# Down projection: results added from PSUM onto the output tiles, narrow weights two to a buffer, three operand kinds stored whole

## The chip, the cores and the metric

One core of a Trainium2 chip runs the kernel. The metric is the device time of one execution in microseconds. The execution that the profile shows is one of its own, recorded by the hardware profiler.

Engines: PE (TensorE) multiplies, with PEld as its weight load; DVE (VectorE), ACT (ScalarE) and POOL (GpSimd) do elementwise work; SP (SyncE) issues all DMAs here. Each engine works through its instructions in a fixed order.

## The reference

A decoder block on x of 2048 positions by 1024 features, float32: a normalised input goes through a combined projection into gated linear attention and a gated short convolution, whose results are mixed and added to x. Then follows the part that the change concerns:

```
h2 = rmsnorm(x, norm2_g[l])
ffn = (jax.nn.silu(h2 @ w_ffn_gate[l]) * (h2 @ w_ffn_up[l])) @ w_ffn_down[l]
x = x + ffn
...
return rmsnorm(x, norm_f_g)
```

The hidden width D_FF is 2816.

## The kernel before

**Layout.** Features lie on the 128 partitions, positions along the free axis, in four blocks of 512 (PB); a half is two blocks. A large matrix product is made of units. A unit takes a 2 by 2 block of weight tiles and two by two blocks of the right operand (feature halves by position blocks) and computes four result tiles of 128 by 512 with seven products in place of eight, in Winograd's form of Strassen's scheme (PRODUCTS, line 36). Each of the seven pairs one weight combination (A11, S1, S2, A12, S3, S4, A22) with one operand combination (B11, T1, T2, B21, T3, B22, T4).

**Precision.** Every float32 operand is split in two fp32r parts: ACT writes the high part (a copy, line 154), DVE the rest (a subtraction, line 155). One step of a product is three matmuls, high by high, high by low and low by high (lines 399 to 401).

**A unit's weights** (unit_weights, line 376). One DMA loads the four raw quarters into one of two raw buffers. POOL forms S1, S2, S3 and S4 in place and in the single buffer s1 (lines 382, 383, 384, 389). Each of the seven is split into a buffer wq; there are 4 of them, each large enough for a weight of 512 columns by two parts.

**A unit's results** (unit, line 403). The accumulators oa and ob are PSUM banks that several products run on in: oa holds product 0, then adds product 2, then 4, then 6; ob holds product 1 and later adds 5; product 3 has a bank of its own. Between those, results are read out: after products 0, 1 and 2 ACT copies oa, ob, oa to c11, c22, c12 (line 419); products 3, 4 and 5 are followed by a DVE addition onto those (line 423); what oa holds after product 6 is c21, which stays in PSUM. A product that adds on a bank has to wait until the read before it is done. With `into` the copies go straight to given tiles.

**The feed-forward part.** For each half, ffn_up (line 923) runs 11 passes m of two units (gate and up), multiplies the two, and makes the operand kinds for the down projection: B11, B21, B22, in some passes B12, and the differences T1 to T4 on POOL. split_later splits each of them on ACT and DVE, as a background task that takes a step every second product, and stores both parts (512 KB) in DRAM, in s_act.

ffn_down (line 956) goes through the 11 passes in four groups that start at GROUPS = (0, 2, 5, 8): the first holds 2 passes, the others 3. At a group's start the operands of its passes are loaded, seven kinds each, into buffers op (28 of them, seven of which hold y during the down projection); seven loads of the second group are sent ahead (EARLY). Each group then runs four units, one for two output rows d0. Group 0 has weights of 256 columns and writes its results into the tiles y (`into`); groups 1 to 3 have weights of 384 columns, and their results are added onto y after the unit (line 1000): c21 from PSUM by DVE, the others by POOL, except that DVE also takes c12 in the last group of the second half. In groups 1 and 2 the residual x1 is loaded and added on POOL (line 1007). The last group of the first half stores y (finished later); in the second half it takes sums of squares (ACT squares, POOL adds, lines 803 to 809), and its last unit is a function of its own, last_unit, with eight plain products and the final norm.

**Operands stored whole.** For the normalised inputs of the in and up projections the kinds in WHOLE (T3, B22, T4) are already stored as one float32 tile (256 KB) and split after loading, in load_whole (line 568): one ACT and one DVE instruction for each. The other kinds are stored split and loaded by load_pair.

**Order.** The text gives the instructions in program order; a scheduler that plans with a timeline places them in each engine's order, taking earlier ones first among those that it believes ready. issue_after(ins) ties what is traced in its block behind an instruction of the same engine. PE runs unit after unit; raw loads and weight splits run ahead of it as far as buffers allow.

Of the kernel before, what the change touches and what calls it, by code (L numbers as in the profile page):

```python
# [10 lines left out]
F32 = mybir.dt.float32  # L11
# [41 lines left out]
def tile_hymba_block(ctx, tc, x, xt, win, wa, wgu, wout, wffn, wdown, wdown_first, small, out):  # L53
# [48 lines left out]
    def scratch(name, n):  # L102
        return [
            [dram.tile([P, PB], F32, name=f"{name}{b}_{i}") for i in range(n)] for b in range(NB)
        ]

    s_kq, s_d, s_v, s_g = scratch("sk", 4), scratch("sd", 2), scratch("sv", 4), scratch("sg", 4)
    s_x1 = scratch("sx", KD)
# [4 lines left out]
            {  # L113
                n: dram.tile([P, 2, PB], F32, name=f"sa{half}_{m}_{n}")
                for n in ("B11", "B12", "B21", "B22", "T1", "T2", "T3", "T4")
# [5 lines left out]
    s_h2 = {n: [dram.tile([P, PB], F32, name=f"sf{n}_{k}") for k in range(4)] for n in LATER}  # L121

    def made_ahead(name, n):
        return dram.tile([P, PB] if n in WHOLE else [P, 2, PB], F32, name=name)

# [222 lines left out]
    def plain_unit(src, ops):  # L348
# [12 lines left out]
        return us  # L361

    def weight_quarter(src):
        n = src.shape[-1]
        h = wqp.tile([P, 2, PB], F32R, name="wq", tag="wq")[:, :, 0:n]
        split(src, h[:, 0, :], h[:, 1, :])
        return h
# [7 lines left out]

    def unit_weights(src):
        raw = raw_weights(src)
        n = src.shape[-1]
        a11, a12, a22, a21 = [raw[:, i, :] for i in range(4)]
        s1 = rawp.tile([P, PB], F32, name="s1", tag="s1", bufs=1)[:, 0:n]  # L380
        w = {"A11": weight_quarter(a11)}
        pool.tensor_tensor(s1, a21, a22, ALU.add)  # L382
        pool.tensor_tensor(a21, a11, a21, ALU.subtract)  # L383
        pool.tensor_tensor(a11, s1, a11, ALU.subtract)  # L384
        w["S1"] = weight_quarter(s1)
        w["S2"] = weight_quarter(a11)
        w["A12"] = weight_quarter(a12)
        w["S3"] = weight_quarter(a21)
        pool.tensor_tensor(a12, a12, a11, ALU.subtract)  # L389
        w["S4"] = weight_quarter(a12)  # L390
        w["A22"] = weight_quarter(a22)
        return w

# [8 lines left out]

    def unit(src, ops, into=None):


        w = unit_weights(src)

        def mul(i, o=None):
# [6 lines left out]
            return o  # L415

        def copied(name, o, at):
            t = tt(name) if into is None else into[at]
            act.activation(t[:], o[:], AF.Copy)  # L419
            return t  # L420

        def plus(t, o):
            dve.tensor_tensor(t[:], o[:], t[:], ALU.add)  # L423
            return t
# [13 lines left out]
        mul(6, oa)  # L438
        if into is not None:
            copied("c21", oa, (1, 0))  # L440
# [499 lines left out]
    def split_later(dst, values):  # L940

        for n, y in values:
            store_split(dst[n], y)
            yield

# [5 lines left out]
    def act_op(half, m, n):  # L951
        o = opp.tile([P, 2, PB], F32R, name="op", tag="op")
        load(o[:].bitcast(F32), s_act[half][m][n][:])
        return o

    def ffn_down(half):
# [6 lines left out]
        for u, m0 in enumerate(GROUPS):  # L963
            ms = range(m0, m0 + (3 if u else 2))
            last = m0 == LAST_GROUP
            if last:
                drain_background()
            ops = {n: [group_op(m, n) for m in ms] for _, n in PRODUCTS}
            if last and half:
# [4 lines left out]
            for d0 in range(0, KD, 2):  # L974
# [19 lines left out]
                if last and half and d0 == KD - 2:  # L994
                    last_unit(src, ops, [act_op(half, m, "B12") for m in ms], y, ssq)
                    break
                for r, j, c, p in unit(src, ops):
                    yy = y[d0 + r, j]
                    eng = dve if p or last and half and r != j else pool
                    eng.tensor_tensor(yy, c[:], yy, ALU.add)  # L1000
                    if last and half:
                        sum_squares(ssq[j], yy, j not in begun)
                        begun.add(j)
                    elif last:
                        store(s_x1[2 * half + j][d0 + r][:], yy)
# [216 lines left out]
```

## Time and profile before

| | us |
|---|---|
| median of 3 runs | 2104.45 |
| lowest, highest | 2103.83, 2107.36 |
| the profiled execution, its own time | 2106.52 |
| its span, first to last instruction | 2104.4 |
| busy: PE, PEld, DVE, ACT, POOL | 2036.8, 1656.3, 1415.8, 998.6, 973.1 |

In the span, the up projection of the first half runs from about 745 to 1180 us and its down projection to about 1400; the second half's up projection follows to about 1835 and its down projection to the end. DMA queues moved 456 MB, all issued by SP.

How to read the lines of the profile: a group or timeline row names the line of the kernel, the engine, the operation, and output<-inputs by tile name (numbers of buffers left out), with partitions by elements, and xN for N instructions. Behind a bar or in brackets stands idle time of the engine just before the instructions, and what ended it: [5.83 <-POOL s L382] is 5.83 us of waiting that ended when POOL's instruction of line 382 on tile s did. Lines 154 and 155 are the helper that splits, so the tile name tells what is split: wq a weight, op an operand, so a result to be stored. In the rows by stage, (xN) is the number of instructions, and the last three numbers are PE's granted clock as a share of full speed, the busy share of the DMA engines and GB/s.

### The profile page before, as it was taken

The page shows a single profiled execution, that of the slowest core. Times are in us where ns is not written, and L with a number is a line of the kernel's source. Part 1 is how long each engine was busy: PE and PEld are TensorE (multiplying, and loading weights), DVE is VectorE, ACT ScalarE, POOL GpSimd, SP SyncE. Part 2 cuts the span into 40 slices and gives each one's busy share as a digit, 9 for nine tenths or more (in the row PEclk, how much of TensorE's full clock was granted, in tenths as well). Part 3 has the DMA queues.
Part 4 walks back from the last instruction along what each step waited for, and adds up shares of the span by engine and source line. Part 5 has one row for each costly group of instructions (what it writes and reads, how often), then busy time and mean ns, then how long its engine had stood idle before and what let it go on. Part 6 is the DMA issues. An engine that isn't in the chain of part 4 may idle for free.

```text
span 2104.4 us, 27023 instructions
## 1 busy us (share of the span) xinstructions
PE 2036.8 (97%) x9193; PEld 1656.3 (79%) x9193; DVE 1415.8 (67%) x2018; ACT 998.6 (47%) x1982; POOL 973.1 (46%) x704
## 2 busy tenths in 40 slices
PE   6999999999999999999999999999999999999996
PEld 4768888877888878788888878787888878877775
DVE  7669786549743786787786665557766677575554
ACT  6555455656542355445444443334544544443343
POOL 3436222222102564464464448865545544437773
PEclk9999999999999999999999999999999999999998
DMA  7349385425686862655545687695554544687672
GB/s 279 127 169 315 130 339 160 147 80 175 201 282 242 316 245 106 232 193 212 212 166 191 260 327 269 235 338 225 188 199 169 200 173 169 221 341 261 240 277 98
DMA packets 189241, 458.14 MB, mean 218 GB/s; under 512 B 19824, under 2 KB 65072, under 8 KB 179504
## 3 DMA queue, kind: packets, MB, share of 16 engines
q1 hardware_dynamic: 189104, 456.43, 60.1%
q8 instruction: 72, 1.18, 0.2%
q14 instruction: 65, 0.53, 0.1%
HBM read 294.34 MB, written 162.00 MB: 217 GB/s over the span
## 4 chain that ended last, share of the span: by engine, by line
PE 72%; DVE 7%; DMA 6%; issue 3%; ACT 2%; POOL 2%; SPq 1%; DVEq 0%; ACTq 0%; POOLq 0%
PE mm L399 20%; PE mm L401 20%; PE mm L400 20%; PE mm L827 3%; PE mm L828 2%; PE mm L830 2%; DVE wq L155 2%; DVE so L155 1%; DMA raw<-in_wdown_dram 1%; DMA op<-sa_T 1%; DMA x<-sx 1%; POOL y L1000 1%; ACT wq L154 1%; DMA sa_T<-so 1%; PE o_ps L751 1%
## 5 line engine op out<-in xcount | busy, mean ns | idle before, releaser
L399 PE MATMUL mm<-op,wq 128*128 128x512 f32 x2499 | 980.7, 394 | 20.1 <-ACT wq L154 8.4
L400 PE MATMUL mm<-op,wq 128*128 128x512 f32 x2499 | 975.8, 391 | 0.7 <-DVE op L155 0.7
L401 PE MATMUL mm<-op,wq 128*128 128x512 f32 x2499 | 965.5, 392 | 10.7 <-DVE wq L155 10.0
L155 DVE TENSOR_TENSOR wq<-raw,wq 128x512 fp32r<-128x512 f32 (+2 forms) x626 | 526.5, 848 | 335.8 <-ACT wq L154 333.4
L154 ACT ACTIVATE wq<-raw 128x512 fp32r<-128x512 f32 (+2 forms) x626 | 363.3, 587 | 551.5 <-PE mm L401 389.8
L399 PEld LDWEIGHTS mm<-op,wq 128*128 128x128 f32 x2499 | 470.8, 188 | 133.9 <-ACT wq L154 14.4
L401 PEld LDWEIGHTS mm<-op,wq 128*128 128x128 f32 x2499 | 470.5, 188 | 119.4 <-DVE wq L155 20.8
L400 PEld LDWEIGHTS mm<-op,wq 128*128 128x128 f32 x2499 | 470.9, 188 | 97.5 <-DVE op L155 1.3
L384 POOL TENSOR_TENSOR raw<-s,raw 128x512 f32<-128x512 f32 (+2 forms) x97 | 127.8, 1318 | 419.2 <-DVE wq L155 398.9
L423 DVE TENSOR_TENSOR c<-mm,c 128x512 f32<-128x512 f32 x267 | 183.0, 685 | 93.2 <-PE mm L401 91.1
L382 POOL TENSOR_TENSOR s<-raw 128x512 f32<-128x512 f32 (+2 forms) x97 | 129.1, 1331 | 212.0 <-DMA raw<-in_wffn_dram 88.0
L389 POOL TENSOR_TENSOR raw<-raw 128x512 f32<-128x512 f32 (+2 forms) x97 | 124.7, 1286 | 126.5 <-DVE wq L155 119.2
L419 ACT ACTIVATE c<-mm 128x512 f32<-128x512 f32 x267 | 154.7, 585 | 36.0 <-PE mm L401 34.5
L809 POOL TENSOR_TENSOR ssx<-ssx,q 128x512 f32<-128x512 f32 x52 | 76.2, 1477 | 154.4 <-ACT q L808 154.3
L383 POOL TENSOR_TENSOR raw<-raw 128x512 f32<-128x512 f32 (+2 forms) x97 | 136.7, 1409 | 4.1
L1000 POOL TENSOR_TENSOR y<-c,y 128x512 f32<-128x512 f32 x66 | 98.9, 1501 | 58.2 <-DVE c L423 56.3
L155 DVE TENSOR_TENSOR so<-t,so 128x512 fp32r<-128x512 f32 x96 | 93.2, 976 | 24.3 <-ACT so L154 24.2
L154 ACT ACTIVATE wq<-s 128x512 fp32r<-128x512 f32 (+2 forms) x97 | 56.8, 585 | 97.4 <-PE mm L401 85.0
L827 PE MATMUL mm<-op,wq 128*128 128x512 f32 x256 | 100.9, 395 | 0.0
L828 PE MATMUL mm<-op,wq 128*128 128x512 f32 x256 | 99.7, 389 | 0.0
L155 DVE TENSOR_TENSOR wq<-s,wq 128x512 fp32r<-128x512 f32 (+2 forms) x97 | 79.9, 823 | 15.1 <-ACT wq L154 14.5
L830 PE MATMUL mm<-op,wq 128*128 128x512 f32 x256 | 79.8, 390 | 0.0
(185 smaller groups left out, 1871.8 us busy)
## 6 DMA issues: line engine op xcount, KB each, us to landing
raw<-in_wffn_dram SPq DMA_DIRECT2D x44, 1024.0 KB, 6.4
sa_T<-so SPq DMA_DIRECT2D x88, 512.0 KB, 5.9
op<-sa_T SPq DMA_DIRECT2D x88, 512.0 KB, 9.5
sa_B<-so SPq DMA_DIRECT2D x69, 512.0 KB, 3.4
op<-sa_B SPq DMA_DIRECT2D x69, 512.0 KB, 9.2
raw<-in_win_dram SPq DMA_DIRECT2D x23, 1024.0 KB, 5.4
raw<-in_wdown_dram SPq DMA_DIRECT2D x24, 768.0 KB, 6.1
sx<-y SPq DMA_DIRECT2D x48, 256.0 KB, 3.1
```

What stands on the lines that cost most here:

```text
L154: last_hi[:] = [act.activation(hi, src, AF.Copy)]
L155: return dve.tensor_tensor(lo, src, hi.bitcast(F32), ALU.subtract)
L382: pool.tensor_tensor(s1, a21, a22, ALU.add)
L383: pool.tensor_tensor(a21, a11, a21, ALU.subtract)
L384: pool.tensor_tensor(a11, s1, a11, ALU.subtract)
L399: pe.matmul(o[:], wh, xh, start=first and k == 0, stop=False, skip_group_check=True)
L400: pe.matmul(o[:], wh, xl, start=False, stop=False, skip_group_check=True)
L401: return pe.matmul(o[:], wl, xh, start=False, stop=k == n - 1, skip_group_check=True)
L419: act.activation(t[:], o[:], AF.Copy)
L423: dve.tensor_tensor(t[:], o[:], t[:], ALU.add)
L827: pe.matmul(o[e, j][:], wh, m[:, 0, :], start=k == 0, stop=False)
L828: pe.matmul(o[e, j][:], wh, m[:, 1, :], start=False, stop=False)
```

## The change

Three parts, and what goes with them:

- In groups 1 to 3 of the down projection unit gets `onto`: DVE adds each of the seven readings of PSUM straight onto the y tile. The copies into c and the later additions on POOL are gone from these groups. The squares, stores and residual additions that follow are the same.
- A weight of 256 columns takes half of a buffer wq, and the next one the other half. A half that is left at the end of a unit isn't used.
- T3, B22 and T4 of the down projection's operands are stored whole in DRAM and loaded by load_whole, which splits them. split_later stores these three first, straight from where they were computed, then splits and stores the others one step at a time. Two functions move up in the text for that.
- In groups 1 to 3 the raw weights of the first unit are loaded ahead of the group's operands, whose loads are tied behind it.

```diff
@@ -104,6 +104,9 @@
             [dram.tile([P, PB], F32, name=f"{name}{b}_{i}") for i in range(n)] for b in range(NB)
         ]
 
+    def made_ahead(name, n):
+        return dram.tile([P, PB] if n in WHOLE else [P, 2, PB], F32, name=name)
+
     s_kq, s_d, s_v, s_g = scratch("sk", 4), scratch("sd", 2), scratch("sv", 4), scratch("sg", 4)
     s_x1 = scratch("sx", KD)
     s_mix = [[dram.tile([P, 2, PB], F32, name=f"sm{b}_{k}") for k in range(4)] for b in range(NB)]
@@ -111,7 +114,7 @@
     s_act = [
         [
             {
-                n: dram.tile([P, 2, PB], F32, name=f"sa{half}_{m}_{n}")
+                n: made_ahead(f"sa{half}_{m}_{n}", n)
                 for n in ("B11", "B12", "B21", "B22", "T1", "T2", "T3", "T4")
             }
             for m in range(NF // 2)
...
@@ -360,9 +360,18 @@
                 us.append((r, j, settled(o, True), False))
         return us
 
+    halves = []
+
     def weight_quarter(src):
+
         n = src.shape[-1]
-        h = wqp.tile([P, 2, PB], F32R, name="wq", tag="wq")[:, :, 0:n]
+        if halves:
+            h = halves.pop()
+        else:
+            h = wqp.tile([P, 2, PB], F32R, name="wq", tag="wq")
+            if n == PB // 2:
+                halves.append(h[:, :, n:])
+            h = h[:, :, 0:n]
         split(src, h[:, 0, :], h[:, 1, :])
         return h
 
@@ -373,8 +382,8 @@
         raw_loads.append(load(raw, src))
         return raw
 
-    def unit_weights(src):
-        raw = raw_weights(src)
+    def unit_weights(src, raw=None):
+        raw = raw_weights(src) if raw is None else raw
         n = src.shape[-1]
         a11, a12, a22, a21 = [raw[:, i, :] for i in range(4)]
         s1 = rawp.tile([P, PB], F32, name="s1", tag="s1", bufs=1)[:, 0:n]
@@ -389,6 +398,7 @@
         pool.tensor_tensor(a12, a12, a11, ALU.subtract)
         w["S4"] = weight_quarter(a12)
         w["A22"] = weight_quarter(a22)
+        halves.clear()
         return w
 
     def product_step(o, w, op, k, first):
@@ -400,10 +410,11 @@
         pe.matmul(o[:], wh, xl, start=False, stop=False, skip_group_check=True)
         return pe.matmul(o[:], wl, xh, start=False, stop=k == n - 1, skip_group_check=True)
 
-    def unit(src, ops, into=None):
-
-
-        w = unit_weights(src)
+    def unit(src, ops, into=None, onto=None, raw=None):
+
+
+
+        w = unit_weights(src, raw)
 
         def mul(i, o=None):
             first = o is None
@@ -414,13 +425,15 @@
             tick()
             return o
 
+        def plus(t, o):
+            dve.tensor_tensor(t[:], o[:], t[:], ALU.add)
+            return t
+
         def copied(name, o, at):
+            if onto is not None:
+                return plus(onto[at], o)
             t = tt(name) if into is None else into[at]
             act.activation(t[:], o[:], AF.Copy)
-            return t
-
-        def plus(t, o):
-            dve.tensor_tensor(t[:], o[:], t[:], ALU.add)
             return t
 
 
@@ -436,7 +449,7 @@
         mul(5, ob)
         plus(c12, ob)
         mul(6, oa)
-        if into is not None:
+        if into is not None or onto is not None:
             copied("c21", oa, (1, 0))
         return [(0, 0, c11, False), (1, 1, c22, False), (0, 1, c12, False), (1, 0, oa, True)]
 
@@ -940,8 +953,12 @@
     def split_later(dst, values):
 
         for n, y in values:
-            store_split(dst[n], y)
-            yield
+            if n in WHOLE:
+                store(dst[n][:], y[:])
+        for n, y in values:
+            if n not in WHOLE:
+                store_split(dst[n], y)
+                yield
 
     def store_split(dst, y):
         o = bx[1].tile([P, 2, PB], F32R, name="so", tag="so")
@@ -949,9 +966,7 @@
         store(dst[:], o[:].bitcast(F32))
 
     def act_op(half, m, n):
-        o = opp.tile([P, 2, PB], F32R, name="op", tag="op")
-        load(o[:].bitcast(F32), s_act[half][m][n][:])
-        return o
+        return (load_whole if n in WHOLE else load_pair)(s_act[half][m][n])
 
     def ffn_down(half):
 
@@ -965,7 +980,13 @@
             last = m0 == LAST_GROUP
             if last:
                 drain_background()
-            ops = {n: [group_op(m, n) for m in ms] for _, n in PRODUCTS}
+            raw = None
+            if u:
+                raw = raw_weights(wdown[4 * u - 4])
+                with tc.issue_after(raw_loads[-1].ins):
+                    ops = {n: [group_op(m, n) for m in ms] for _, n in PRODUCTS}
+            else:
+                ops = {n: [group_op(m, n) for m in ms] for _, n in PRODUCTS}
             if last and half:
                 begun = set()
                 ssq = [
@@ -994,10 +1015,10 @@
                 if last and half and d0 == KD - 2:
                     last_unit(src, ops, [act_op(half, m, "B12") for m in ms], y, ssq)
                     break
-                for r, j, c, p in unit(src, ops):
-                    yy = y[d0 + r, j]
-                    eng = dve if p or last and half and r != j else pool
-                    eng.tensor_tensor(yy, c[:], yy, ALU.add)
+                onto = {(r, j): y[d0 + r, j] for r in range(2) for j in range(2)}
+                unit(src, ops, onto=onto, raw=None if d0 else raw)
+                for r, j in ((0, 0), (1, 1), (0, 1), (1, 0)):
+                    yy = onto[r, j]
                     if last and half:
                         sum_squares(ssq[j], yy, j not in begun)
                         begun.add(j)
```

2 lines of the change are left out of this document (removed).

## The prediction

> **What bounds the kernel now.** I read the page's first lines, then PE's busy time by stage, then the timelines of the few stretches where PE is not full.
>
> ```profile
> span 2104.4 us, 27023 instructions
> PE 2036.8 (97%) x9193; PEld 1656.3 (79%) x9193; DVE 1415.8 (67%) x2018; ACT 998.6 (47%) x1982; POOL 973.1 (46%) x704
> ```
>
> PE is busy for 97% of the span, and the change leaves every matmul in place. What can be won is the rest, 2104.4 - 2036.8 = 67.6 us, and only the part of it that lies where the change works. The stages (columns: stretch, its length, busy time and instructions of PE, PEld, DVE, ACT, POOL, then the granted clock, the DMA share, GB/s):
>
> ```profile
> 745.00:1180.00 435.00, 428.27 (x1869) 350.99 (x1869) 330.65 (x384) 215.45 (x373) 231.75 (x155) 1.00 0.52 188
> 1240.00:1390.00 150.00, 148.99 (x653) 121.51 (x652) 80.58 (x114) 54.61 (x109) 109.93 (x86) 1.00 0.75 287
> 1600.00:1700.00 100.00, 100.00 (x443) 82.79 (x442) 65.94 (x78) 46.87 (x83) 55.23 (x38) 1.00 0.49 173
> ```
>
> The third row is the yardstick: 443 matmuls in 100.00 us without a gap, 0.2257 us each. In any stretch, length minus matmuls times 0.2257 is PE time lost, including the slow restart after a gap. Groups 1 to 3 of the first half's down projection (second row) lose 1.0 us of idle time in 150: there is little to win there. The losses that the change can reach are these:
>
> ```profile
> 835.00:855.00 20.00, 17.13 (x67) 13.36 (x66) 20.00 (x27) 12.37 (x22) 10.89 (x7) 0.91 0.59 213
> 1225.00:1235.00 10.00, 7.69 (x31) 5.35 (x30) 5.72 (x10) 4.27 (x11) 4.63 (x6) 1.00 0.48 192
> 1870.00:1880.00 10.00, 7.69 (x31) 5.36 (x30) 6.58 (x11) 4.99 (x12) 4.91 (x6) 1.00 0.47 189
> 1920.00:1930.00 10.00, 8.25 (x36) 6.39 (x35) 4.72 (x6) 2.57 (x6) 9.92 (x9) 1.00 0.37 129
> 1960.00:1970.00 10.00, 8.26 (x27) 5.86 (x26) 2.08 (x4) 1.80 (x4) 5.67 (x5) 0.83 1.02 407
> 2030.00:2040.00 10.00, 7.41 (x33) 5.68 (x32) 5.35 (x10) 5.69 (x11) 5.82 (x5) 1.00 0.38 154
> ```
>
> By the yardstick: 835 to 855 loses 20 - 67 x 0.2257 = 4.9 us (DVE is busy for all of it); the end of group 0 loses 3.0 us in each half (1225, 1870); the second half's later groups lose 1.9, 3.9 and 2.6 us. That is 19.3 us in all.
>
> **The change part by part.**
>
> Narrow weights, two to a buffer. Group 0 of the down projection has weights 256 wide and products of 6 matmuls, 1.35 us. With 4 buffers a weight can be split once the product four before it has ended: it has three products, 4.1 us, of lead. In pairs, the seven weights of a unit fill four buffers, so the next unit's first pair is free after product 1 of this one and leads by five products, 6.8 us. The raw weight buffer is also released earlier, by about those three products. What PE waits for there:
>
> ```profile
> 1226.62 0.50 PE L399 MATMUL mm<-op,wq 128*128 128x512 f32 x1 [0.78 <-DVE y L423]
> 1229.80 0.50 PE L399 MATMUL mm<-op,wq 128*128 128x512 f32 x1 [1.51 <-ACT wq L154]
> ```
>
> Two thirds of the idle time is a weight that came late, which more lead answers; the other third is an eviction into y, which it does not. Of 3.0 us per half I take 2.0: **-4.0 us** for both (bounds: 0, if the raw load is what is late, and -6.0).
>
> Additions off POOL. The groups that change:
>
> ```profile
> L1000 POOL TENSOR_TENSOR y<-c,y 128x512 f32<-128x512 f32 x66 | 98.9, 1501 | 58.2 <-DVE c L423 56.3 <-DMA x<-sx 1.8
> L423 DVE TENSOR_TENSOR c<-mm,c 128x512 f32<-128x512 f32 x267 | 183.0, 685 | 93.2 <-PE mm L401 91.1 <-ACT c L419 0.7
> L419 ACT ACTIVATE c<-mm 128x512 f32<-128x512 f32 x267 | 154.7, 585 | 36.0 <-PE mm L401 34.5
> ```
>
> There are 12 units less the last one of group 3 in the second half: 23. Each drops three ACT evictions (1.8 us) and its additions from c (three, 4.5 us of POOL; in the last group of the second half one of them is DVE's), and gains up to three DVE evictions from PSUM (2.1 us). POOL and ACT do not bound, so the busy time itself is worth nothing; what counts is who queued behind it:
>
> ```profile
> 1917.79 1.54 POOL L1000 TENSOR_TENSOR y<-c,y 128x512 f32<-128x512 f32 x1 [1.80 <-DMA x<-sx]
> 1919.30 2.53 POOL L1007 TENSOR_TENSOR y<-x,y 128x512 f32<-128x512 f32 x2
> 1924.40 0.53 ACT L154 ACTIVATE wq<-s 128x384 fp32r<-128x384 f32 x1 [5.83 <-POOL s L382]
> 1964.86 0.52 ACT L154 ACTIVATE wq<-raw 128x384 fp32r<-128x384 f32 x1 [2.97 <-DMA raw<-in_wdown_dram]
> 2031.67 0.63 ACT L805 ACTIVATE ssx<-y 128x512 f32<-128x512 f32 x1 [2.17 <-POOL y L1000]
> ```
>
> At 1920 the weight sum s stands on POOL behind the additions. Two L1000 additions leave that chain (about 3 us), the residual additions L1007 and their loads stay; of 1.9 us I take 1.5. At 1960 the wait is a raw load landing while the DMA engines are full; fewer bytes per operand help it a little: 1.0 of 3.9. At 2030 a square on ACT waits for the POOL addition, and weight splits and evictions stand behind it on ACT; after the change y comes straight from DVE and no eviction is on ACT: 2.0 of 2.6. With 0.5 of the first half's 1.0 us the term is **-5.0 us** (bounds 0 and 1.9 + 3.9 + 2.6 + 1.0 = -9.4).
>
> Evictions onto y by DVE. Two more matmul groups per unit now wait for a DVE read of their bank: product 2 for that of product 0, product 4 for that of product 2. The slack is one product, 9 x 0.2257 = 2.03 us, against 0.685 us and whatever stands before it on DVE (lo parts of weights and operands, which wait for ACT). PE's own waits give the price:
>
> ```profile
> PE mm L399 <- ACT c L419: 7.0, 6, 2.6
> PE mm L399 <- DVE c L423: 2.5, 2, 1.9
> PE mm L399 <- DVE y L423: 1.6, 2, 0.8
> ```
>
> One in three L423 instructions holds a bank back, 89 gates for 2.5 us, 0.028 us each; on y in group 0 it is 8 gates for 1.6 us, 0.2 each; on ACT 178 gates for 7.0 us, 0.039 each. The 46 moved gates therefore cost between 46 x (0 - 0.039) = -1.8 and 46 x 0.2 = 9.2 us. DVE's load after the change is nearest to that of the up projection (330.65 of 435 us, 76%): 80.58 us in 150, plus some 30 evictions at 0.685 and 18 operand splits at 0.84, is 116, or 78%. So I take the c row: **+1.3 us**.
>
> Three kinds stored whole. In the up projection 66 splits go (ACT and DVE each), their stores and later loads halve to 256 KB, and 66 splits come back behind the loads at the start of the down groups: nine at each of six starts, six at each of two. Rows:
>
> ```profile
> L155 DVE TENSOR_TENSOR so<-t,so 128x512 fp32r<-128x512 f32 x96 | 93.2, 976 | 24.3 <-ACT so L154 24.2
> L155 DVE TENSOR_TENSOR op<-op 128x512 fp32r<-128x512 f32 x24 | 19.6, 842 | 0.0
> L154 ACT ACTIVATE op<-op 128x512 fp32r<-128x512 f32 x24 | 14.2, 622 | 1.2 <-DMA op<-shT 1.2
> op<-sa_T SPq DMA_DIRECT2D x88, 512.0 KB, 9.5
> ```
>
> Up: per pass of two units DVE loses 3 x 0.976 = 2.9 us, which is worth something only where DVE is full: of the 4.9 us at 835 I take 2.0, and 1.0 for the small gaps later: **-3.0 us** (bounds 0 and -6.0). The whole stores wait on SP for POOL's differences with later loads behind them; raw loads run about a unit ahead of their use, so I cost that at nothing, and if that lead is gone it is one late raw load as at 1960, 3.9 us.
>
> Down: the trace of before has two starts with twelve whole operands each. Out of the first I quote the stretch, out of the second the stretch and PE's waits in it:
>
> ```profile
> 265.00:305.00 40.00, 40.00 (x198) 32.20 (x197) 30.83 (x51) 23.59 (x55) 8.70 (x7) 1.00 1.02 394
> 1435.00:1455.00 20.00, 17.61 (x76) 13.86 (x76) 17.49 (x24) 13.42 (x25) 7.46 (x6) 1.00 0.47 179
> PE mm L399 <- ACT c L419: 1.7, 1, 1.7
> PE mm L400 <- DVE op L155: 0.7, 1, 0.7
> PE mm L399 <- ACT op L154: 0.3, 1, 0.3
> ```
>
> The first cost PE nothing, the second 1.0 us on the operands and 2.7 with the eviction that was late behind them. For twelve operands then 0 to 2.7 us; scaled to nine or six, 66/12 = 5.5 such starts: 0 to 14.8 us. DVE, at 54% in these groups before, has spare time that the second start (87%) had not, so I go to between the two plain prices, 0.58 per twelve: **+3.2 us**.
>
> Raw weights ahead of operands. At the second start of a group in the first half:
>
> ```profile
> 1288.10 0.33 SPq L146 DMA_DIRECT2D raw<-in_wdown_dram  x1
> 1291.05 0.32 SPq L146 DMA_DIRECT2D op<-sa_B  x1
> ```
>
> The raw load already goes first, since its buffer comes free earlier than the operands' buffers. The 21 operand loads that are now tied behind it lose nothing: 0.
>
> Sum: -4.0 - 5.0 + 1.3 - 3.0 + 3.2 = **-7.5 us**. Against the profiled span that is 2096.9; the run that was profiled took about 2 us more than its span and lies within the 2103.83 to 2107.36 of the three runs, so I subtract from the median, 2104.45: **2097.0 us**.
>
> A rule that bears on the splits: the Trainium skill, "SBUF — State Buffer", section "Who interferes with whom", says that a DVE instruction with two inputs in SBUF and a GpSimd instruction that reads SBUF exclude each other for a whole instruction. Both the removed additions and the new operand splits are of that kind, an eviction from PSUM is not. By it a split that meets one POOL instruction would cost up to its own time and 1.5 us more, nine of them about 14 us more per start, and the sum would come out slower. The measured 842 ns mean speaks for few such meetings.
>
> **The rivals.**
>
> Slower: ACT and DVE blocked at the head of their queues by a late operand. The operand's hi split stands in ACT's order behind its load, with the weights of the coming products and, on DVE, the evictions behind it; before, only PE waited for these loads, and no PE wait on them shows. For it: loads take 9.5 us in the median, DMA is full at the starts, the 1435 start lost 2.7 us. Against it: ACT waited 1.2 us in all for 24 such loads. At 2.7 us for each of eight starts: -12.0 + 1.3 + 21.6 = +10.9, or 2115 us. It decides once a start loses more than (12.0 - 1.3)/8 = 1.3 us.
>
> No change: the losses in the down groups only move to the next late thing, the raw load at 1960 or the residual loads at 1920. Then the first two terms fall away: -3.0 + 1.3 + 3.2 = +1.5, or 2106 us. For it: two of the five down losses end in a DMA. Against it: the 2030 loss does not.
>
> Larger gain: every bound of the gains, no price at the starts: -6.0 - 9.4 - 6.0 + 1.3 = -20.1, or 2084 us. For it speaks the first start (265), against it that DVE gets busier.
>
> **How the numbers follow.** Forecast 0.46, slower 0.29, no change 0.15, larger gain 0.10. A run can tell about 0.2%, 4.2 us, from no change. Faster holds the larger gain and nearly all of the forecast: 0.55; within: the rest and the no-change case, 0.16; slower 0.29. The forecast's own range, with its gains or its prices at half their way to the bounds, is 2089 to 2105. The range over the cases runs from 2086, which leaves out part of the larger gain, to 2115, the price of the slower case.
>
> **What would show it.** Right: no idle time before wq at the end of group 0 in either half; no L1000-like additions on POOL and ACT's squares no longer waiting for POOL near 2030; DVE near 78% in the down groups and PE waits on its evictions under 2 us in all; op splits (66 more) with little waiting for DMA. Wrong: ACT idle until an op load at the group starts, with PE waits on wq behind it; PE waits for DVE evictions of half a microsecond and more in many units; a DVE mean for op splits well over 1 us.

## The result, and the profile after

The changed kernel takes 2089.69 us in the median of 4 runs (2087.49 to 2091.39) against 2105.9 us (2103.83 to 2109.0) for the kernel before on the same chip: a ratio of 0.9915 with a 95% interval of 0.9898 to 0.9932. By the ratio that is 17.9 us less, between 14.3 and 21.5; the two medians lie 16.2 us apart. The forecast had 7.5 us: the sign is right, the time is within the range (2086 to 2115), the gain was set at less than half.

The page's first lines after:

```profile
span 2085.4 us, 26960 instructions
PE 2029.7 (97%) x9193; PEld 1656.5 (79%) x9193; DVE 1429.7 (69%) x2084; ACT 965.5 (46%) x1913; POOL 881.3 (42%) x638
```

The two spans differ by 19.0 us. Of that, 11.9 us are idle time of PE (67.6 to 55.7 us). The other 7.1 us are busy time, though the matmuls are the same: some ran slower. Up to 2.9 us of it is the clock, which was granted at half for six stretches, 34.7 us in all, before and for five, 28.9 us, after.

To see where, I ordered PE's matmuls by their start in the timeline of each profile and compared the start of the n-th; in the feed-forward part all kernels here run the same matmuls in the same order, but for two to four neighbouring pairs in the second up projection. The stages below are bounded by such numbers, which run 11 ahead of a matmul's place among the 9193 of the trace. First seven stretches of before (columns as in the prediction; in order, to within a few matmuls: 3800 to 4400, 5480 to 5600, 5600 to 6200, 8200 to 8400, 8520 to 8560, 8680 to 8720, 8900 to 9040), then the same matmuls after:

```profile
829.99:973.48 143.49, 138.92 (x602) 113.44 (x601) 110.19 (x134) 73.70 (x127) 73.42 (x49) 0.99 0.60 214
1220.24:1250.74 30.50, 28.19 (x121) 22.16 (x120) 18.04 (x31) 14.61 (x34) 9.55 (x11) 1.00 0.71 266
1250.74:1389.30 138.56, 137.55 (x601) 112.06 (x600) 73.92 (x103) 48.93 (x98) 105.34 (x82) 1.00 0.73 280
1846.95:1896.72 49.77, 47.29 (x201) 36.88 (x200) 35.46 (x57) 25.13 (x56) 19.35 (x20) 1.00 0.86 337
1924.30:1935.72 11.42, 9.67 (x41) 7.12 (x40) 5.84 (x9) 4.91 (x10) 8.47 (x9) 1.00 0.07 23
1963.31:1976.19 12.88, 11.26 (x41) 8.56 (x40) 4.35 (x6) 3.32 (x7) 8.19 (x7) 0.87 0.91 364
2017.37:2052.33 34.96, 32.37 (x141) 26.04 (x140) 18.03 (x25) 18.34 (x35) 22.54 (x19) 1.00 0.61 239
```
```profile
832.76:973.22 140.46, 137.30 (x602) 112.31 (x600) 99.54 (x123) 66.84 (x115) 72.28 (x50) 1.00 0.54 192
1218.88:1246.09 27.21, 27.21 (x121) 22.53 (x120) 16.55 (x30) 12.78 (x29) 8.74 (x11) 1.00 0.65 243
1246.09:1384.26 138.17, 137.58 (x601) 112.05 (x600) 106.23 (x161) 49.85 (x96) 70.44 (x55) 1.00 0.64 233
1842.06:1888.28 46.22, 45.63 (x202) 37.47 (x201) 35.93 (x58) 23.37 (x53) 20.34 (x20) 1.00 0.80 297
1915.47:1924.54 9.07, 9.07 (x41) 7.51 (x40) 4.68 (x10) 2.13 (x5) 3.86 (x3) 1.00 0.19 59
1951.95:1962.22 10.27, 9.87 (x42) 7.20 (x40) 10.27 (x11) 6.00 (x12) 6.76 (x5) 1.00 0.45 172
2003.19:2035.59 32.40, 32.37 (x142) 26.05 (x140) 27.36 (x40) 21.84 (x41) 18.00 (x15) 1.00 0.44 161
```

The end of group 0 (second row), the stretch that was at 1920 (fifth) and the one at 2030 (last) now run practically without a gap. In the third row DVE is busy for 106.23 of 138.17 us, 77%, and PE still idles for only 0.6 us.

PE's waits for the high part of a weight in the whole profile before (one row); three rows of PE's waits in the whole profile after; and its only wait after around the end of the first half's group 0 (1190 to 1250 us):

```profile
PE mm L399 <- ACT wq L154: 8.4, 7, 1.7
```
```profile
PE mm L409 <- ACT c L436: 3.6, 4, 1.7
PE mm L409 <- DVE y L429: 1.5, 4, 0.6
PE mm L409 <- ACT wq L154: 1.5, 2, 1.2
```
```profile
PE mm L409 <- DVE y L429: 0.6, 1, 0.6
```

Waits of a product's first matmul for the high part of a weight fell from 8.4 to 1.5 us, for ACT's copies from 7.0 to 3.6. The new evictions onto y hold PE for 1.5 us in all. The groups that carry the change:

```profile
L429 DVE TENSOR_TENSOR y<-mm,y 128x512 f32<-128x512 f32 x185 | 126.9, 687 | 83.7 <-PE mm L411 83.3
L1028 POOL TENSOR_TENSOR y<-x,y 128x512 f32<-128x512 f32 x32 | 53.1, 1658 | 46.3 <-DVE y L429 37.4 <-DVE op L155 4.5 <-DMA x<-sx 4.3
L155 DVE TENSOR_TENSOR op<-op 128x512 fp32r<-128x512 f32 x90 | 74.1, 850 | 3.3 <-ACT op L154 3.2
L154 ACT ACTIVATE op<-op 128x512 fp32r<-128x512 f32 x90 | 52.5, 621 | 7.3 <-DMA op<-sa_T 3.9 <-DMA op<-shT 1.4 <-DMA op<-sa_B 1.3
op<-sa_T SPq DMA_DIRECT2D x44, 512.0 KB, 7.1
```

DVE reads PSUM onto y 185 times in place of 47 (24 in group 0 and 23 in line 1000), the 66 POOL additions from c are gone, and there are 66 more op splits, at 0.85 us on DVE; before all 90 op splits together ACT waited 7.3 us, mostly for their loads. The loads of split operands land in 7.1 us, down from 9.5.

### The profile page after: what moved, and what is told of

Read it like the earlier page. It is cut to its first block, busy times and chain, and to the rows that moved or that the text cites. A ratio compares the mean times of both kernels' runs of the same rounds, so it can differ in the third digit from the quotient of the medians.

```text
span 2085.4 us, 26960 instructions
## 1 busy us (share of the span) xinstructions
PE 2029.7 (97%) x9193; PEld 1656.5 (79%) x9193; DVE 1429.7 (69%) x2084; ACT 965.5 (46%) x1913; POOL 881.3 (42%) x638
## 4 chain that ended last, share of the span: by engine, by line
PE 80%; DVE 6%; DMA 3%; ACT 2%; issue 1%; POOL 1%; SPq 0%; DVEq 0%; ACTq 0%; POOLq 0%
PE mm L409 24%; PE mm L411 24%; PE mm L410 24%; PE mm L840 1%; PE mm L841 1%; PE mm L843 1%; DVE op L155 1%; DVE wq L155 1%; DVE h L536 1%; DMA op<-shT 1%; PE o_ps L764 1%; PE o_ps L766 1%; DMA ee<-sd 0%; DMA sm<-hi 0%; DVE y L429 0%
## 5 line engine op out<-in xcount | busy, mean ns | idle before, releaser
L155 DVE TENSOR_TENSOR wq<-raw,wq 128x512 fp32r<-128x512 f32 (+2 forms) x626 | 508.7, 818 | 281.0 <-ACT wq L154 278.5
L429 DVE TENSOR_TENSOR c<-mm,c 128x512 f32<-128x512 f32 x198 | 135.8, 686 | 76.9 <-PE mm L411 75.0
L429 DVE TENSOR_TENSOR y<-mm,y 128x512 f32<-128x512 f32 x185 | 126.9, 687 | 83.7 <-PE mm L411 83.3
L436 ACT ACTIVATE c<-mm 128x512 f32<-128x512 f32 x198 | 115.4, 586 | 16.1 <-PE mm L411 14.4
L155 DVE TENSOR_TENSOR wq<-s,wq 128x512 fp32r<-128x512 f32 (+2 forms) x97 | 84.9, 875 | 2.9 <-ACT wq L154 2.1
L155 DVE TENSOR_TENSOR op<-op 128x512 fp32r<-128x512 f32 x90 | 74.1, 850 | 3.3 <-ACT op L154 3.2
```

Source lines behind the costliest of these rows:

```text
L155: return dve.tensor_tensor(lo, src, hi.bitcast(F32), ALU.subtract)
```

## The experiments

Each table entry is the length of a stage in one profile minus its length in the kernel before (first column, us), worked out from the matmul starts as above. "control" is the kernel before profiled again: it shows by how much two profiles of one kernel differ, 1.0 us at most in the up projections and 0.4 us in the down projections. Stages up to matmul 6480 belong to the first half of the positions (the end of its last group and the load of the second half's operands lie in 6200 to 6480), the later ones to the second half. A star marks a stage in which that kernel ran one stretch at half clock, explained below the table.

```
matmuls     what             before  | control  after | pairs   onto    whole  | whole+onto no_whole no_pairs
3800-5200   up projection     326.2* |   1.0    -4.4  |  -0.1*   0.0    -4.4   |   -4.4       0.7*    -3.7*
5200-5600   group 0            94.6  |   0.1    -3.0  |  -2.2    0.1     1.5   |    0.9      -2.2      0.9
5600-6200   groups 1 to 3     138.6  |   0.0    -0.4  |   1.0   -1.4     3.5   |    0.0      -1.9     -0.5
6200-6480   end, next half     67.3  |  -0.4     1.3  |  -0.4   -0.7     2.7*  |    0.1      -0.7      0.3
6480-8200   up projection     390.6  |  -0.2    -1.4  |   0.9*   1.4    -1.4   |   -1.1       1.0*    -0.7
8200-8400   group 0            49.8  |   0.0    -3.5  |  -2.7    1.6*    0.4   |    1.0      -2.2      0.4
8400-8680   group 1, 2         66.6  |   0.0    -3.1  |  -0.8   -3.1    -1.0   |   -2.6      -2.0     -2.0
8680-8720   (was 1963)         12.9* |   0.0*   -2.4  |  -2.5   -3.1    -1.8   |   -2.5      -3.1     -2.5
8720-8900   group 2, 3         41.2  |   0.0     0.0  |  -0.1   -0.4     0.6   |    0.1      -0.4      0.1
8900-9040   group 3            35.0  |   0.0    -2.6  |   1.6*  -3.0     0.5   |   -2.6      -3.0     -2.6
3800-9040                    1222.6  |   0.7   -19.5  |  -5.2   -8.6     0.6   |  -11.1     -13.8    -10.2
measured ratio                       |         0.9915 | 0.9974 0.9965  0.9997  |  0.9955     0.9932   0.9944
```

Ratios are to the kernel before on the same chip, whose median was 2105.9 to 2109.4 us; all intervals are within 0.0017 of the ratio on either side.

**Stretches at half clock.** Now and then the granted clock fell to a half for 3.41 us, which costs 1.7 us where PE is busy. In the stages of the table there are 17 such stretches in the sixteen profiles, and each follows right on 3.41 us in which PE was idle for 1.5 to 2.6 us. The first two rows are of before, the loss at 1963 (PE busy for 1.68 of 3.40 us, clock 1.00) and what follows it (clock 0.50); the third is of before after its gap of 2.6 us near 2039, the fourth of copies_dve, a kernel described below, after its gap at the same place, 2.7 us. At full clock 16 matmuls fall into such a row, at half 8 or 10:

```profile
1962.90:1966.30 3.40, 1.68 (x6) 0.79 (x6) 1.51 (x2) 0.52 (x1) 1.48 (x2) 1.00 1.02 408
1966.30:1969.70 3.40, 3.40 (x8) 2.75 (x9) 0.00 (x0) 0.00 (x0) 3.03 (x3) 0.50 1.03 404
2041.40:2044.80 3.40, 3.40 (x16) 2.81 (x16) 0.90 (x1) 2.58 (x5) 2.66 (x3) 1.00 0.36 144
2038.90:2042.30 3.40, 3.40 (x10) 2.65 (x9) 1.10 (x3) 0.89 (x2) 1.95 (x2) 0.51 0.47 186
```

So a gap of one size can cost 1.7 us more or not, and a stage that differs by about that much may differ in the clock alone. The changed kernel has no such stretch in these stages, the kernel before has two: 3.4 of the 19.5 us are the clock, 1.7 of them the loss at 1963 and 1.7 in the first up projection. Control has none in that projection and is no shorter there, so the second 1.7 us can't be booked as a lasting gain.

**One part alone: only_pairs, only_onto, only_whole.** Each is the kernel before with the lines of one part of the diff: `halves` in weight_quarter and unit_weights; `onto` in unit and ffn_down; made_ahead for s_act, split_later and act_op. The core of each:

```diff
+            if n == PB // 2:
+                halves.append(h[:, :, n:])
...
+            if onto is not None:
+                return plus(onto[at], o)
...
+        return (load_whole if n in WHOLE else load_pair)(s_act[half][m][n])
```

> The kernel before with only the pairing of narrow weights. Theory (the forecast's step, with the size that the trace after shows): the end of group 0 loses about 3 us less in each half, nothing changes elsewhere: -6 us, ratio near 0.997. Rival: at the end of group 0 the gain comes from fewer split instructions and bytes (operands stored whole), so pairing alone gives within 1 us of before.

> The kernel before with only the additions from PSUM onto y by DVE. Theory: the second half's groups 1 to 3 lose 8 to 10 us less (the stretches that began at 1920, 1960 and 2030 in the kernel before), group 0 and the up projection stay: -9 us. Rival: the stretch at 1960 belongs to the operand loads and stays, and evictions that wait on DVE take some back: -4 us.

> The kernel before with only the three kinds stored whole (no raw load moved). Theory: the up projection of the first half gains 4 us and the group starts cost 0 to 3 us: -4 to -1 us. Rival 1: the group starts gain too, since 22% fewer bytes stand before the raw loads: -8 us. Rival 2 (the forecast's slower case): ACT and DVE are held at the group starts: +3 us or more.

Pairing: 0.9974 (0.9964 to 0.9984), and the two group 0 stages lose 4.9 us as the theory said. Additions from PSUM: 0.9965 (0.9952 to 0.9978), 7.4 us; the stages that were named are 9.6 us shorter, and the second half's group 0, with a stretch at half clock, is 1.6 us longer. Storing whole: 0.9997 (0.9987 to 1.0007), and the table shows why it is nothing: the first up projection gains 4.4 us, as expected, and the first half's down projection gives 1.5, 3.5 and 2.7 us back, 7.6 in all, 1.7 of it half clock; the second half's stages gain 2.7 in all.

The three parts together would give 0.9974 x 0.9965 x 0.9997 = 0.9936, 13.5 us; the change gives 0.9915. With these intervals the ratios alone hardly tell the two apart, but the table does: in the first half's groups 0 to 3 (5200 to 6200), where control agrees to 0.1 us and nothing ran at half clock, the parts alone add up to +2.4 us and the change gives -3.4. They are not independent.

One thing fits no theory: only_pairs, which touches neither POOL nor the loads of groups 1 to 3, is 2.5 us shorter at 1963 (1.7 of it the half clock that is not there) and, between matmuls 8520 and 8560, the stretch at 1920, 1.5 us shorter too. only_whole, which leaves the additions on POOL, is even 2.4 us shorter between 8520 and 8560, all that was lost there. POOL's timeline in that stretch, first the weight sum in the kernel before (three of the four instructions ahead of it are in the prediction), then only_pairs:

```profile
1923.36 1.01 POOL L382 TENSOR_TENSOR s<-raw 128x384 f32<-128x384 f32 x1
```
```profile
1914.62 1.30 POOL L1009 TENSOR_TENSOR y<-c,y 128x512 f32<-128x512 f32 x1
1917.02 1.54 POOL L1016 TENSOR_TENSOR y<-x,y 128x512 f32<-128x512 f32 x1 [1.09 <-DVE y L1009]
1918.52 1.28 POOL L1009 TENSOR_TENSOR y<-c,y 128x512 f32<-128x512 f32 x1
1919.78 1.32 POOL L390 TENSOR_TENSOR s<-raw 128x384 f32<-128x384 f32 x1
```

The same work stands in another order, with matmul 8520 at nearly the same time (1924.2 and 1924.3): the sum s starts at 1919.78, behind two additions in a row, not at 1923.36 behind four. The order that the scheduler made shifted with the earlier stage.

**The kernel before once more: control.** No edit.

> The kernel before, unchanged, for a second profile of it. If the losses of the second half's groups 1 and 2 (the stretches at 1920 and 1960) belong to the kernel, they are there again, 2 and 3.5 us. If they belong to that one execution, they are not, and what the change gained there was never the additions' doing.

2110.15 us in its one execution, and the two stretches are there again to within 0.1 us, the half clock at 1963 too. So they belong to the kernel before and not to one execution of it. At 1920 the order of instructions, which different edits move, is shown above; at 1963 what every edit takes away is first of all the half clock.

**Which queue matters: adds_dve and copies_dve.**

```diff
adds_dve:
-                    eng = dve if p or last and half and r != j else pool
+                    eng = dve
copies_dve (units of groups 1 to 3 only):
-            act.activation(t[:], o[:], AF.Copy)
+            dve.tensor_copy(t[:], o[:])
```

> The kernel before with the additions of line 1000 all on DVE, still from c, and the ACT copies kept. If what helps is that POOL no longer stands before the weight sums and the squares, this gives most of the gain of adding from PSUM, -6 us or more, although DVE does 66 more instructions of two SBUF inputs. If the ACT copies and the longer way over c matter, it gives 0 to -2 us, or a loss by DVE's load.

> The kernel before, with the copies to c in groups 1 to 3 of the down projection made by DVE in place of ACT; the additions stay on POOL. If the loss near 2030 comes from evictions that stand on ACT behind the squares (and weight splits), it goes here, 2.5 us between matmuls 8900 and 9040. If it comes from the squares' wait for POOL's additions, it stays. In all -5 to 0 us.

adds_dve: 0.9988 (0.9977 to 0.9998), between the two expectations; it gains 1.9 and 2.3 us at the two stretches above but only 0.5 in group 3. copies_dve: 0.9995 (0.9983 to 1.0007), and group 3 is 1.8 us longer, not 2.5 shorter; 1.7 of that is half clock, so the loss itself simply stays. PE's waits near there, first of adds_dve (2018 to 2059 us), then of copies_dve (2015 to 2057 us):

```profile
PE mm L399 <- ACT c L419: 3.3, 2, 2.2
```
```profile
PE mm L399 <- DVE c L420: 3.0, 2, 2.7
```

The wait for the copy follows the copy to whichever engine makes it. The timeline shows why. In the kernel before, out of the rows of DVE, ACT and PE:

```profile
2035.53 0.63 ACT L808 ACTIVATE q<-y 128x512 f32<-128x512 f32 x1 [1.78 <-DVE y L1000]
2037.37 0.57 DVE L155 TENSOR_TENSOR wq<-raw,wq 128x384 fp32r<-128x384 f32 x1 [1.87 <-ACT wq L154]
2037.86 0.68 DVE L1000 TENSOR_TENSOR y<-mm,y 128x512 f32<-128x512 f32 x1
2038.57 0.63 ACT L808 ACTIVATE q<-y 128x512 f32<-128x512 f32 x1 [0.82 <-DVE y L1000]
2039.11 1.06 ACT L419 ACTIVATE c<-mm 128x512 f32<-128x512 f32 x2
2039.73 0.50 PE L399 MATMUL mm<-op,wq 128*128 128x512 f32 x1 [2.59 <-ACT c L419]
```

The copies stand on ACT behind squares, and the squares wait for additions that DVE makes in the kernel before already; DVE's addition in turn stands behind a low part that waits for ACT. POOL's addition, for which the square at 2031.67 waits in the rows of the prediction, is an early link of this chain. With it on DVE (adds_dve) the two squares still wait, 1.50 and 0.47 us. With the copy on DVE (copies_dve) it stands there behind the same late low part:

```profile
2035.46 0.57 DVE L155 TENSOR_TENSOR wq<-raw,wq 128x384 fp32r<-128x384 f32 x1 [1.87 <-ACT wq L154]
2037.24 1.28 DVE L420 COPY c<-mm 128x512 f32<-128x512 f32 x2
```

So neither single queue of my reading is the cause there, but a chain that passes from ACT to DVE and back; only the direct way, without the copy and the second addition, takes the 2.6 us away.

**What covers the splits at the group starts: whole_onto, whole_adds_dve, whole_copies_dve.** The first is only_whole with only_onto's lines; the others are only_whole with the one-line edits above.

> The kernel before with two parts: the additions from PSUM by DVE, and the three kinds stored whole; no pairing, no raw load moved. If the parts only add up, 0.9965 and 0.9997 give 0.996. If the additions off ACT and POOL are what covers the splits at the group starts, the 3 to 7 us that the whole operands cost in the first half's down projection alone are not there, and it gives 0.993 to 0.994.

> The three kinds stored whole, with line 1000's additions all on DVE and the copies left on ACT. If POOL's additions slow DVE's splits and that is the cost at the starts, it goes here although DVE does the additions itself (mean of a 384 wide weight's lo part well under the 0.84 us that it has with the kinds stored whole alone). If ACT's copies are the cause, the 3.5 and 2.7 us stay.

> As copies_dve, with the three kinds stored whole as well. If what the whole operands cost at the first half's group starts (3.5 us between matmuls 5600 and 6200, 2.7 between 6200 and 6480, when done alone) is ACT's copies standing behind the operand splits, it goes here. If it is DVE held up by POOL's additions and having too much to do, it stays or grows, since DVE gets the copies on top.

whole_onto: 0.9955 (0.9942 to 0.9967), and the 3.5 and 2.7 us at the starts are 0.0 and 0.1. whole_adds_dve: 0.998 (0.9966 to 0.9993), the starts cost 1.3 and -0.3. whole_copies_dve: 1.0035 (1.0022 to 1.0049), the starts cost 6.2 and 1.6.

These are differences to the kernel before, and the edits to the additions and copies gain or lose there by themselves. The price of storing whole is the difference to the kernel with the same edit that stores split. In the first half's down projection (5200 to 6480) it is 7.6 us alone, or 5.9 without the half clock; 9.4 with the copies on DVE; 4.3 with the additions on DVE (against copies_dve and adds_dve); 3.0 with the additions from PSUM; and 2.7 in the changed kernel (after less no_whole). ACT's copies were not the cause; taking the additions off POOL is most of the cure there, even when DVE does them itself, but the price does not go to nothing. In the second half's down projection the same differences run from -1.2 us (alone) to 2.7 (additions on DVE) in no such order, with half clocks among them, so the dependence is shown for the first half only. The low part of a 384 wide weight and of an operand on DVE, between 1256 and 1400 us; in order: before (one row), only_whole, whole_adds_dve, whole_copies_dve, the changed kernel:

```profile
L155 DVE TENSOR_TENSOR wq<-raw,wq 128x384 fp32r<-128x384 f32 x60 | 47.2, 798 | 43.4 <-ACT wq L154 43.4
```
```profile
L156 DVE TENSOR_TENSOR wq<-raw,wq 128x384 fp32r<-128x384 f32 x59 | 51.6, 886 | 25.9 <-ACT wq L155 25.8
L156 DVE TENSOR_TENSOR op<-op 128x512 fp32r<-128x512 f32 x25 | 23.3, 975 | 2.1 <-ACT op L155 2.1
```
```profile
L156 DVE TENSOR_TENSOR wq<-raw,wq 128x384 fp32r<-128x384 f32 x61 | 43.4, 714 | 20.8 <-ACT wq L155 20.7
L156 DVE TENSOR_TENSOR op<-op 128x512 fp32r<-128x512 f32 x24 | 17.0, 749 | 1.6 <-ACT op L155 1.6
```
```profile
L156 DVE TENSOR_TENSOR wq<-raw,wq 128x384 fp32r<-128x384 f32 x57 | 51.0, 896 | 15.4 <-ACT wq L155 15.3
L156 DVE TENSOR_TENSOR op<-op 128x512 fp32r<-128x512 f32 x24 | 22.7, 975 | 1.1 <-ACT op L155 1.1
```
```profile
L155 DVE TENSOR_TENSOR wq<-raw,wq 128x384 fp32r<-128x384 f32 x61 | 40.1, 659 | 2.3 <-ACT wq L154 2.3
L155 DVE TENSOR_TENSOR op<-op 128x512 fp32r<-128x512 f32 x20 | 17.4, 900 | 0.0
```

The same subtraction takes 0.80 us before, 0.89 with POOL's additions and the operand splits, 0.71 with the additions on DVE, 0.66 in the changed kernel. only_whole and whole_adds_dve have the same splits and differ in the engine of the additions alone, so it is POOL's additions that make 0.89 out of 0.71. Some 60 of them in a down projection's 140 us make 60 x (0.80 - 0.66) = 8 us of DVE time less than before, a part of the room that the operand splits need, which take 17.4 us there.

**One part left out: no_rawfirst, no_whole, no_pairs.** The changed kernel less one part each:

```diff
no_rawfirst:
-                raw = raw_weights(wdown[4 * u - 4])
-                with tc.issue_after(raw_loads[-1].ins):
no_whole:
-        return (load_whole if n in WHOLE else load_pair)(s_act[half][m][n])
+        return load_pair(s_act[half][m][n])
no_pairs:
-            if n == PB // 2:
-                halves.append(h[:, :, n:])
```

> The changed kernel without the raw weights loaded ahead of the operands. Theory of the forecast (the raw load goes first anyway): same as the changed kernel, ratio to before near 0.9915. Rival: the raw load's place is what takes the cost of the operands stored whole away at the group starts, so without it 3 to 7 us come back, ratio near 0.994 to 0.995.

> The changed kernel with the three kinds stored split again. If the parts add up, what is left is pairing and additions, 0.9974 x 0.9965 = 0.994, and storing whole is worth 2.5 thousandths in the changed kernel although it is worth nothing alone: 4 us in the up projection and no cost at the starts. If storing whole is worth nothing here either, it gives 0.9915.

> The changed kernel without the pairing of narrow weights. If pairing is worth here what it is worth alone (0.9974, some 5 us), it gives 0.994 of the kernel before. If group 0 of the changed kernel needs it more, because the whole operands' splits now stand among its weights, it is worth 8 to 10 us: 0.9955, with the loss between matmuls 5200 and 5600 and between 8200 and 8400.

no_rawfirst: 0.9909 (0.9894 to 0.9924), the same as the changed kernel: that part does nothing. no_whole: 0.9932 (0.9917 to 0.9946): storing whole, worth nothing alone, is worth 0.9932 - 0.9915 = 0.0017 or 3.6 us here. By the table it gains 5.1 + 2.3 us in the two up projections (3.4 of these half clock in no_whole) and costs 2.7 us in the first half's down projection, while the second half's gets 0.9 us shorter. no_pairs: 0.9944 (0.9931 to 0.9957): pairing is worth 0.0029, 6 us, by the runs; by the table the two group 0 stages are 4.0 + 3.9 = 7.9 us longer without it, against 4.9 us that it gains alone. Both are differences of ratios with intervals of 0.0013 to 0.0017 to each side, so their sizes are rough, and the 3.6 us are not clear of noise.

**More kinds, fewer kinds: more_whole and two_whole.** The changed kernel with another set of kinds for the down projection's operands:

```diff
-WHOLE = ("T3", "B22", "T4")
+more_whole: ("B21", "T3", "B22", "T4")
+two_whole:  ("B22", "T4")
```

> The changed kernel with a fourth kind, B21, stored whole too: 22 splits more leave the up projection and come back at the group starts, where they are due one product earlier. If a split at the start costs nothing once the additions are off ACT and POOL, it is as fast as the changed kernel or 1 us faster. If every split there has the price that I put on it (0.05 us each and more), it loses 1 to 4 us at the starts.

> The changed kernel with two kinds stored whole (B22 and T4, due last) in place of three. If the third kind's splits still cost something at the starts, this is 1 to 3 us faster than the changed kernel, ratio 0.990 to 0.991, provided the up projection keeps its 5 us. If three kinds are free at the starts and a part of the up projection's gain goes with the third, it is 1 to 2 us slower, ratio near 0.992.

more_whole: 0.9944 (0.9928 to 0.9961), slower than the changed kernel by 0.0029, 6 us. Its profile is 9.4 us longer over the table's stages, and it loses in both group 0 stages too (1.5 and 2.1 us). Its groups 1 to 3 of the first half and PE's waits from 1200 to 1400 us:

```profile
1247.84:1389.07 141.23, 137.98 (x602) 111.88 (x601) 111.50 (x168) 51.28 (x99) 68.83 (x55) 1.00 0.59 213
```
```profile
PE mm L412 <- DVE wq L156: 1.7, 2, 1.5
PE mm L410 <- DVE c L430: 1.1, 1, 1.1
PE mm L411 <- DVE op L156: 1.1, 1, 1.1
```

Against the changed kernel's 138.17 us and 106.23 us of DVE, 5 us more of DVE work and 3 us more time: PE waits for DVE, and B21 is due a product earlier than the other three. two_whole: 0.9906 (0.989 to 0.9921), not to be told from the changed kernel; its stages differ by -1.1 in groups 1 to 3 and +1.3 in the first up projection: what the third kind costs at the starts it gains before them. The fourth kind costs more than it gains. None of the runs is clearly faster than the changed kernel.

## Why the prediction fell short

**The step that failed is the size of the gains: from each loss I took a part, where the runs show that nearly the whole of it closes.** By the ratios of the parts alone, each to within 2 to 3 us, additions from PSUM gave 7.4 us where the forecast had 5.0 - 1.3 = 3.7, pairing 5.5 where it had 4.0, and storing whole 0.6 where it had -0.2: 13.5 us, so 6.0 of the 10.4 us that the forecast lacks. The other 4.4 us appear only with the parts together. That is a second failed step: every term was priced against the trace of before, as if the other parts of the change were not there.

**Bound and place: right.** PE bounds, and all of the gain lies in the stretches named: by the table 3800 to 5200 (-4.4), both ends of group 0 (-3.0 and -3.5) and the three losses of the second half (-3.1, -2.4, -2.6) make -19.0 of the -19.5 us.

**Narrow weights: mechanism right, size too small.** I took -4.0 and set 6.0 as the bound. Alone it gave -4.9, in the changed kernel 6.6 against before and 7.9 against no_pairs. I had excluded the third of the idle time that was an eviction into y, yet the gap all but closed: after, the wait there is one of 0.6 us. The bound of 6.0 was too low as well: the whole operands would make group 0 worse without pairing (+1.5 and +0.4 in only_whole).

**Additions off POOL: place right, size and mechanism partly wrong.** I took 1.5 + 1.0 + 2.0 + 0.5 = 5.0 of 9.4; in the stages of these losses it came to -3.1 (1920), -2.4 (1963), -2.6 (2030) and -0.4 in the first half, 8.5. At 1920 the chain through POOL was right as a description, but the loss was a matter of order, of which pairing alone removes 1.5 us and storing whole alone all. At 1963 I gave the raw load little hope and 1.0 us. By the yardstick 3.9 us were lost there, but 1.7 of them were the half clock behind the gap and only 1.6 the gap itself in the trace; once the gap shrank (to 0.4 us in the changed kernel) the half clock went as a whole, as with every single edit. At 2030 I blamed the squares' wait for POOL: adds_dve takes POOL out of that wait and gains only 0.5 us; the squares that stand just ahead of the late copies wait for DVE.

**Evictions by DVE: a little too dear.** +1.3 forecast; PE waited for y on DVE for 1.5 us in all, against 1.6 us with 24 of them before. DVE's load was foreseen (78%, measured 77%).

**Kinds stored whole: size right, dependence missed.** The first up projection gave -4.4 against -3.0; how much of that is the half clock that before happened to have there is open. The price at the starts, +3.2, was too small for the part alone (7.6 us in the first half, 5.9 without the half clock; the second half's down projection got 1.2 us shorter, by the half clock that before has in it) and somewhat too large for the change, where no_whole gives 2.7 less 0.9. The two starts that I scaled it from have POOL busy for 8.70 of 40 and 7.46 of 20 us; the down groups of before have 109.93 of 150. whole_adds_dve and whole_copies_dve show that this price depends on what else the change puts on POOL and DVE. The rival with ACT blocked at the head of its queue did not happen: ACT waited 7.3 us for 90 operands in all, and moving the copies off ACT made only_whole worse.

The Trainium skill, "SBUF — State Buffer", section "Who interferes with whom", says that a DVE instruction with two SBUF inputs and a GpSimd instruction that reads SBUF shut each other out. I let it stand beside the sum, and used it only against the new splits. The means 0.80, 0.89, 0.71 and 0.66 us agree with it: the subtraction has two SBUF inputs, and it got shorter when POOL's additions went, while the eviction from PSUM stayed at 0.685 to 0.687 us. It worked here on the gain's side too. The 14 us more per start that I worked out by the rule as the worst case did not come: in the changed kernel the first half's down projection is 2.7 us longer for the splits.

**Raw weights first: right,** nothing.

In sum, by the stages of the changed kernel against before: where I had costed 12.0 us of gains, they came to 6.6 + 8.5 + 4.4 = 19.5, 3.4 of it half clock, and the stages that are left balance out (1.3 - 1.4). The costs set at 4.5 us are inside these figures and can't be read off them; for them the kernels with one part left out are the measure.

## What to carry to other kernels

Cost the parts of a change together, not each against the kernel before: work moved to an engine is cheap or dear by what else the change takes from that engine, or from one whose work slows it. When measuring a part, compare with the kernel that has all the rest, not with the first one. In this case the gaps of 2 to 3 us at which a queue held up a chain mostly closed or stayed; when a change rebuilds that queue, take the whole gap as likely, not half of it. And profile the neighbours: a loss that an unrelated edit removes belongs to the order of instructions or to the clock, not to the part that was meant to cure it. Read the granted clock of a stretch before explaining 1.7 us in it.

## What was not expected of the hardware

A DVE subtraction of 384 columns with both inputs in SBUF took 0.66 to 0.90 us in the mean, by how much POOL and DVE itself had to do beside it; DVE's additions from PSUM took 0.68 to 0.69 us in every kernel. A gap of PE of 1.5 to 2.6 us could be followed by 3.41 us at half clock or by none. The splits of a fourth kind, 5 us more of DVE in a stretch of 141 us in which it was then 79% busy, cost 3 us there: an engine's share over a stage says little about the few microseconds in which its work is due.
